# A feed-forward product of a fused transformer layer, with two of eight pairs of k-tiles in seven products for eight

## The chip, the cores and the metric

One core of a Trainium2 chip. The time is device microseconds of one execution; lower is better. The kernel before was run three times.

## The reference

One layer on 256 tokens of width 2048 in float32: an input projection, three kinds of attention, gates, an output projection, residual and layer norm, a feed-forward part, residual and layer norm, and a gated input. What the change touches is the feed-forward part (D = 2048, F = 5632):

```python
a, b = jnp.split(h @ w_ffn_in, 2, axis=-1)
f = (jax.nn.silu(a) * b) @ w_ffn_out
h = layer_norm(ALPHA * h + f, ln2_g, ln2_b)
```

The split and the product with Silu are what the kernel's lines 835 to 844 compute: chunk c of the first half is paired with chunk 11 + c.

## The kernel before

**Products.** TensorE has float32 products in three passes: each operand is split into a high part (`ACT.activation` Copy into a rounded type, line 140) and a low part (`DVE.tensor_sub`, line 141), and lines 208 to 210 sum high x high, low x high and high x low into one PSUM bank. The activations are stationary (128 k-rows by 128 tokens), the weights stream, 512 columns at a time. `gemm` loads weights in groups of two k-tiles (512 KB, line 151) through three `raw` buffers, splits them into four `whi` and four `wlo` buffers, and runs each group for both token halves. So ScalarE and VectorE do one split of 128x1024 for each 12 matmuls.

**Around the norms** a list of `LONG1` to `LONG3` groups is finished one token half before the other, so that the norm of one half lies beside matmuls of the other. Groups beyond four in such a list take their split tiles from a spare pool (`spare`); it is the first group of the list that does. For chunk 0 of the feed-forward part that pool is `k4b` (line 836).

**The feed-forward part.** `hT` holds the normed input in d-major halves (eight tiles of the pool `k4`). For each of 11 chunks of 512 columns: a product, Silu into `g` (ScalarE, line 839), a second product, their product (VectorE, line 843), and for each token half four transposes on TensorE (`to_dmajor`, line 239), whose result is split into `actT` (`k4h`, `k4l`). `actT` stays in SBUF for all 44 k-tiles. The second product (`add_and_norm`, `ffn_out`) has four chunks of 44 k-tiles.

**Order.** Each engine works through one queue in order; the order of each is set when the program is built, by priorities that follow the program text and by when a tile of a pool is free. All weight loads go through SyncE's queue.

**PSUM.** Eight banks: four of the pool `acc`, four of `scp` (transposes and small products).

Of the kernel before, what the change touches and what calls it, by code (L numbers as in the profile page):

```python
# [52 lines left out]
# the attention part of w_in in chunks of columns that one PSUM bank holds  # L53
# [12 lines left out]
# shape-only constants, one array of P rows  # L66
# [51 lines left out]
def build(ctx: ExitStack, tc: tile.TileContext, A: dict):  # L118
# [37 lines left out]
    # Work on the side: generators whose steps go between the groups of a product; each  # L156
    # yields how many groups its next step waits.
# [55 lines left out]

    class Halves:
        """d-major activations [P, n, S] in halves, in tiles of four blocks."""
# [13 lines left out]
        def put(self, k, n, half, src, hi_from=None):  # L229
            """Blocks k..k+n-1 of one token half from src [P, n, P]."""  # L230
# [4 lines left out]
    def to_dmajor(X, k0, src, half):  # L235
        """src [P tokens, 512] -> four blocks of X."""
        tp = sc_tile()
        for i in range(4):
            PE.transpose(tp[:, i * P:(i + 1) * P], src[:, i * P:(i + 1) * P], ident)  # L239
        X.put(k0, 4, half, tp.rearrange("p (n t) -> p n t", n=4))  # L240
# [13 lines left out]
    with ExitStack() as at:  # L254
# [16 lines left out]
        def load_x(k):  # L271
            """x^T up to block k, as the first product comes to it."""
# [562 lines left out]
    for c in range(11):  # L835
        ps = gemm(A["ffn_in"][c], hT, KT, 512, sizes=[[2] * LONG3] if c == 0 else (), spare=[k4b] * (LONG3 - 4))
        a = g_tile()
        for h in range(2):
            ACT.activation(a[:, h, :], ps[h], AF.Silu)  # L839
# [71 lines left out]
```

## Time and profile before

| | |
|---|---|
| runs, us | 1628.68, 1626.96, 1627.76 (median 1627.76) |
| the profiled execution: span, us | 1627.7 |
| TensorE busy | 99% of the span, granted clock 0.999 |
| VectorE, ScalarE busy | 56%, 45% |
| DMA | 310 MB, mean 191 GB/s |

The profile gives the span of one execution, from its first to its last instruction; no other time of that execution is listed, and the span is equal to the median of the runs. Busy time is that of instructions running, not waiting; a matmul is listed with its whole length, 0.39 us, though the next one starts after 0.23 us, so for TensorE the starts in the timeline are what counts. In the timeline, a bracket gives the idle time before an instruction and what ended it.

### The profile page before, as it was taken

How to read it: one execution, taken by the hardware profiler on the slowest of the kernel's cores; microseconds unless marked ns; L12 is line 12 of the kernel's file. 1: busy time of each engine (PE TensorE's matmuls, PEld its weight loads, DVE VectorE, ACT ScalarE, POOL GpSimd, SP SyncE). 2: the span in 40 equal slices, each digit the busy share in tenths (PEclk: the TensorE clock that was granted, in tenths of full speed). 3: DMA queues.
4: the chain of work that ended last, by engine and by line, in shares of the span. 5: the costliest groups of instructions: out<-in, count | busy, mean ns of one | idle time of the engine just before them, and what ended most of it. 6: DMA issues, size and time to landing. Idle time of an engine off the chain costs nothing. (4 is left out here: it accounts for less than half of the span.)

```text
span 1627.7 us, 19843 instructions
## 1 busy us (share of the span) xinstructions
PE 1612.1 (99%) x7581; PEld 1348.2 (83%) x7581; DVE 909.0 (56%) x1183; ACT 733.5 (45%) x917; POOL 17.9 (1%) x38
## 2 busy tenths in 40 slices
PE   9999999999999999999999999999999999999998
PEld 7777899988888888888888888888888888888787
DVE  5679765554646464556755454454454545545764
ACT  5455555554444444444444444444444433433343
POOL 1000000010000000000000000000000100000000
PEclk9999999999999999999999999999999999999999
DMA  7664653567666666677466666666666766666474
GB/s 261 183 193 154 208 160 111 168 205 228 192 193 185 194 193 192 191 232 222 150 196 191 186 193 193 184 192 187 189 190 193 234 194 194 194 194 198 148 232 131
DMA packets 90158, 310.26 MB, mean 191 GB/s; under 512 B 10320, under 2 KB 11472, under 8 KB 90064
## 3 DMA queue, kind: packets, MB, share of 16 engines
q1 hardware_dynamic: 88784, 304.81, 62.1%
q0 software_dynamic: 1280, 4.20, 0.9%
q8 instruction: 59, 0.97, 0.2%
q14 instruction: 35, 0.29, 0.1%
HBM read 306.86 MB, written 2.10 MB: 190 GB/s over the span
## 5 line engine op out<-in xcount | busy, mean ns | idle before, releaser
L141 DVE TENSOR_TENSOR wlo<-raw,whi 128x1024 fp32r<-128x1024 f32 (+2 forms) x572 | 683.1, 1196 | 668.4 <-ACT whi L140 663.9
L140 ACT ACTIVATE whi<-raw 128x1024 fp32r<-128x1024 f32 (+2 forms) x572 | 593.4, 1038 | 790.6 <-PE acc L209 680.0
L208 PE MATMUL acc<-whi,k4h 128*128 128x512 f32 (+2 forms) x2220 | 856.1, 386 | 2.2 <-ACT k4h L140 1.3
L210 PE MATMUL acc<-wlo,k4h 128*128 128x512 f32 (+2 forms) x2220 | 850.8, 383 | 2.1 <-DVE wlo L141 2.1
L209 PE MATMUL acc<-whi,k4l 128*128 128x512 f32 (+2 forms) x2220 | 851.3, 383 | 0.6 <-DVE k4l L141 0.6
L208 PEld LDWEIGHTS acc<-whi,k4h 128*128 128x128 f32 x2220 | 417.5, 188 | 81.4 <-ACT k4h L140 2.3
L210 PEld LDWEIGHTS acc<-wlo,k4h 128*128 128x128 f32 x2220 | 417.2, 188 | 78.9 <-DVE wlo L141 3.1
L209 PEld LDWEIGHTS acc<-whi,k4l 128*128 128x128 f32 x2220 | 417.5, 188 | 76.5 <-DVE k4l L141 1.3
L140 ACT ACTIVATE k4h<-sc 128x512 fp32r<-128x512 f32 (+1 forms) x62 | 33.2, 538 | 29.5 <-PE sc L239 22.3
L141 DVE TENSOR_TENSOR k4l<-sc,k4h 128x512 fp32r<-128x512 f32 (+1 forms) x62 | 36.4, 615 | 5.2 <-ACT k4h L140 5.0
L360 ACT ACTIVATE p<-p,nm 128x128 f32<-128x128 f32 (+1 forms) x40 | 17.8, 446 | 10.0 <-DVE nm L358 10.0
L239 PE MATMUL sc<-ident,g 128*128 128x128 f32 x120 | 19.1, 283 | 1.1 <-DVE g L843 1.1
L239 PEld LDWEIGHTS sc<-ident,g 128*128 128x128 f32 x120 | 12.6, 140 | 7.4 <-DVE g L843 4.1
L251 ACT ACTIVATE g<-acc 128x512 f32<-128x512 f32 x24 | 14.1, 589 | 5.8 <-PE acc L210 5.8
L734 DVE TENSOR_TENSOR g<-g,acc 128x512 f32<-128x512 f32 x24 | 16.4, 684 | 0.4
L571 PE MATMUL sc<-wlo,blk 128*30 128x256 f32 x64 | 15.7, 279 | 0.4 <-DVE wlo L141 0.4
L570 PE MATMUL sc<-whi,blk 128*30 128x256 f32 x64 | 16.0, 283 | 0.0
L140 ACT ACTIVATE wh<-raw 128x1024 fp32r<-128x1024 f32 x9 | 9.6, 1062 | 13.7 <-PE acc L209 5.2
L839 ACT ACTIVATE g<-acc 128x512 f32<-128x512 f32 x22 | 12.9, 589 | 5.3 <-PE acc L210 5.3
L843 DVE TENSOR_TENSOR g<-g,acc 128x512 f32<-128x512 f32 x22 | 15.0, 683 | 0.3
L209 PE MATMUL acc<-wh,k4l 128*128 128x512 f32 x36 | 14.3, 398 | 0.3 <-DVE k4l L141 0.2
L141 DVE TENSOR_TENSOR wl<-raw,wh 128x1024 fp32r<-128x1024 f32 x9 | 11.0, 1223 | 6.3 <-ACT wh L140 6.3
(209 smaller groups left out, 530.6 us busy)
## 6 DMA issues: line engine op xcount, KB each, us to landing
raw<-ffn_in SPq DMA_DIRECT2D x176, 512.0 KB, 3.6
raw<-gate SPq DMA_DIRECT2D x96, 512.0 KB, 3.6
raw<-ffn_out SPq DMA_DIRECT2D x88, 512.0 KB, 4.2
raw<-att_c SPq DMA_DIRECT2D x40, 512.0 KB, 4.4
raw<-att_f SPq DMA_DIRECT2D x48, 384.0 KB, 3.3
raw<-w_out SPq DMA_DIRECT2D x32, 512.0 KB, 4.2
raw<-ple_gate SPq DMA_DIRECT2D x32, 512.0 KB, 4.3
raw<-cmp SPq DMA_DIRECT2D x16, 512.0 KB, 4.3
```

Source lines behind the costliest of these rows:

```text
L140: ACT.activation(hi, src, AF.Copy)
L141: DVE.tensor_sub(lo, src, hi.bitcast(F32))
L208: PE.matmul(o, xh[:, c], h, start=(k == 0), stop=False)
L209: PE.matmul(o, xl[:, c], h, start=False, stop=False)
L210: PE.matmul(o, xh[:, c], l, start=False, stop=(k == kt - 1))
L239: PE.transpose(tp[:, i * P:(i + 1) * P], src[:, i * P:(i + 1) * P], ident)
L251: ACT.activation(G[name][:, h, :], ps[h], AF.Sigmoid)
L360: ACT.activation(p[:, c], p[:, c], AF.Exp, bias=nm[:, h:h + 1], scale=-1.0, accum_out=rs[:, h:h + 1])
L570: PE.matmul(ph[:2 * NCMP, :256], b, hi[:, l, :], start=first, stop=False)
L571: PE.matmul(ph[:2 * NCMP, :256], b, lo[:, l, :], start=False, stop=last)
L734: DVE.tensor_mul(g[:, h, :], g[:, h, :], ps[h])
L843: DVE.tensor_mul(a[:, h, :], a[:, h, :], ps[h])
```

## The change

Chunk 0 stays as it was (its spare tiles now come from `k4`). Chunks 1 to 10 take both their products at once, in `pair_gemm`: a 2 x 2 block product of two token halves by two chunks of columns (a is chunk c, b is chunk 11 + c), in pairs of k-tiles. Six of the eight pairs do the four block products of two k-tiles each, 24 matmuls. In pairs 2 and 4 (`SEVEN`) the two k-tiles are the inner dimension of a 2 x 2 by 2 x 2 block product, and seven products with sums of blocks (the Winograd form of Strassen's scheme) take the place of eight: 21 matmuls. The sums of activation blocks are made once, behind the first norm (`keep_pairs`, `Forms.put`); those of the weights for each chunk on VectorE (lines 276 to 278), from 1 MB of weights in `raw8`; those of the results at the end of pair 4 and of the chunk (lines 295 to 303). Four banks sum the four outputs, and the other four the products that several outputs share; the two pools swap roles from chunk to chunk.

For room the activations are not kept in SBUF: each chunk's are copied out of PSUM whole (line 967), stored to DRAM (line 969), and the first chunk of the second product loads them and splits them (`act_first`, lines 978 to 982). The pool `k4b` is closed before chunk 0 and the pool `fw` of `pair_gemm` stands in its place; a new one opens behind it.

```diff
+SEVEN = (2, 4)
...
+        def put(self, p, raw):
+
+            i = self.at[p]
+            if i // 2 == len(self.t):
+                self.t.append(tuple(self.pool.tile([P, 8, P], F32R, name=f"xf{x}", tag="k4") for x in "hl"))
+            a = [[raw[:, k, h * P:(h + 1) * P] for k in range(2)] for h in range(2)]
+            s = self.pool.tile([P, 4, P], F32, name="xs", tag="k4")
+            DVE.tensor_add(s[:, 0, :], a[1][0], a[1][1])
+            DVE.tensor_sub(s[:, 1, :], s[:, 0, :], a[0][0])
+            DVE.tensor_sub(s[:, 2, :], a[1][0], a[0][0])
+            DVE.tensor_sub(s[:, 3, :], a[0][1], s[:, 1, :])
+            j = 4 * (i % 2)
+            halves(s, *(t[:, j:j + 4, :] for t in self.t[i // 2]))
...
+    def pair_gemm(a, b, X, F, kt, pool, banks):
...
+        own, other = banks
+        c = [[own() for _ in range(2)] for _ in range(2)]
...
+        for p in range(np_):
+            raw = pool.tile([P, 4, 512], F32, name="raw8", bufs=3)
+            nc.sync.dma_start(raw[:, 0:2, :], b[:, 2 * p:2 * p + 2, :])
+            nc.sync.dma_start(raw[:, 2:4, :], a[:, 2 * p:2 * p + 2, :])
+            x = [[tuple(t[:, hs[h]] for t in X(2 * p + k)) for k in range(2)] for h in range(2)]
+            if p not in F.at:
+                w = [split(raw[:, 2:4, :], "", wp, 2), split(raw[:, 0:2, :], "", wp, 2)]
+                for h in range(2):
+                    for j in range(2):
+                        for k in range(2):
+                            product(c[h][j], x[h][k], w[j][k], p == 0 and k == 0, p == np_ - 1 and k == 1)
+                tick()
+                continue
+            t = [wp.tile([P, 1024], F32, name="raw", bufs=3).rearrange("p (k w) -> p k w", k=2) for _ in range(2)]
+            DVE.tensor_tensor(t[0], raw[:, 0:1, :].broadcast_to([P, 2, 512]), raw[:, 1:3, :], op=ALU.subtract)
+            DVE.tensor_sub(t[1][:, 0, :], raw[:, 1, :], t[0][:, 1, :])
+            DVE.tensor_sub(t[1][:, 1, :], raw[:, 3, :], t[1][:, 0, :])
+            b22, b11, b21 = split(raw[:, 1:4, :], "d", pool, 3, bufs=1)
+            t3, t1 = split(t[0], "t", pool, 2)
+            t2, t4 = split(t[1], "t", pool, 2)
+            first, stop = not m, p == last
...
+            product(m[1], x[0][0], b11, first, stop)
+            product(c[0][0], x[0][1], b21)
+            product(c[0][1], F(p, 3), b22)
+            product(m[7], F(p, 2), t3, first, stop)
+            product(m[5], F(p, 0), t1, first, stop)
+            product(m[6], F(p, 1), t2, first, stop)
+            product(c[1][0], x[1][1], t4)
+            if stop:
+                e = [g_tile(), g_tile()]
+                ACT.copy(e[0][:, 0, :], m[1])
+                DVE.tensor_add(e[0][:, 1, :], e[0][:, 0, :], m[6])
+                DVE.tensor_add(e[1][:, 0, :], e[0][:, 1, :], m[7])
+                DVE.tensor_add(e[1][:, 1, :], e[1][:, 0, :], m[5])
+                DVE.tensor_add(e[0][:, 1, :], e[0][:, 1, :], m[5])
+            tick()
+        for h in range(2):
+            for j in range(2):
+                DVE.tensor_add(e[h][:, j, :], e[h][:, j, :], c[h][j])
+        return e
...
+    part.close()
+    spilled = []
+    with tc.tile_pool(name="fw", bufs=2) as fw:
+        for c in range(11):
+            banks = (sc_tile, acc_tile) if c % 2 else (acc_tile, sc_tile)
+            if c == 0:
...
+            else:
+                e = pair_gemm(A["ffn_in"][c], A["ffn_in"][11 + c], hT, F, KT, fw, banks)
+                for h in range(2):
+                    ACT.activation(e[h][:, 0, :], e[h][:, 0, :], AF.Silu)
+                    DVE.tensor_mul(e[h][:, 0, :], e[h][:, 0, :], e[h][:, 1, :])
+                g = [e[h][:, 0, :] for h in range(2)]
+            t = k4.tile([P, 4, S], F32, name="act", tag="k4")
+            for h in range(2):
+                to_dmajor(None, 4 * c, g[h], h, lambda h, k0, tp: ACT.copy(t[:, :, h * P:(h + 1) * P], tp), banks[0])
+            d = dram.tile([P, 4, S], F32, name="actd")
+            nc.sync.dma_start(d, t)
+            spilled.append(d)
...
+    def act_first(k):
+
+        while len(actT.t) <= k // 4:
+            c = len(actT.t)
+            raw = wp.tile([P, 1024], F32, name="raw", bufs=3)
+            raw = raw.rearrange("p (k t) -> p k t", k=4)
+            nc.sync.dma_start(raw, spilled[c])
+            actT.add(k4 if 3 <= c < 7 else k4b)
+            halves(raw, *actT.t[c])
+        return actT(k)
```

**Where instructions stand.** The first place is TensorE's queue at the first feed-forward product, before (`wh4_6718` and `wl4_6719` are the split first weights of chunk 0, in spare tiles):

```order
L210 MATMUL acc_6476<-wlo_6521,k4h_5925 128x512
L208 MATMUL acc_6715<-wh4_6718,k4h_6575 128x512
L209 MATMUL acc_6715<-wh4_6718,k4l_6576 128x512
L210 MATMUL acc_6715<-wl4_6719,k4h_6575 128x512
...
L209 MATMUL acc_6715<-whi_6736,k4l_6578 128x512
L239 MATMUL sc_6681<-ident_73,y_5945 128x128 x4
L210 MATMUL acc_6715<-wlo_6737,k4h_6577 128x512
L239 MATMUL sc_6690<-ident_73,y_5946 128x128 x4
```

and the same place with the change (`wh4_6747`, `wl4_6748` are the same weights):

```order
L212 MATMUL acc_6478<-wlo_6523,k4h_5927 128x512
L331 MATMUL sc_6687<-ident_73,y_5947 128x128 x4
L331 MATMUL sc_6696<-ident_73,y_5948 128x128 x4
L331 MATMUL sc_6706<-ident_73,y_5949 128x128 x4
L331 MATMUL sc_6716<-ident_73,y_5950 128x128 x4
L210 MATMUL acc_6744<-wh4_6747,k4h_6577 128x512
L211 MATMUL acc_6744<-wh4_6747,k4l_6578 128x512
L212 MATMUL acc_6744<-wl4_6748,k4h_6577 128x512
```

All sixteen transposes of the second token half's norm now stand ahead of the product that had them among its matmuls. On ScalarE the split of those first weights stood ahead of every copy of the first token half's norm:

```order
L140 ACTIVATE whi_6520<-raw_6519 128x1024
L140 ACTIVATE wh4_6718<-raw_6717 128x1024
L140 ACTIVATE k4h_6575<-sc_6590 128x4x128
L140 ACTIVATE k4h_6577<-sc_6599 128x4x128
L140 ACTIVATE whi_6724<-raw_6723 128x1024
```

and with the change (`xc` are the whole copies of pairs 2 and 4, `xfh` the high halves of their sums):

```order
L142 ACTIVATE k4h_6581<-sc_6706 128x4x128
L936 COPY xc_6608<-sc_6696 128x2x128
L142 ACTIVATE k4h_6583<-sc_6716 128x4x128
L936 COPY xc_6619<-sc_6706 128x2x128
L142 ACTIVATE xfh_6723<-xs_6725 128x512
L142 ACTIVATE wh4_6747<-raw_6746 128x1024
L142 ACTIVATE xfh_6723<-xs_6732 128x512
```

The split of the first weights moved behind the second token half's norm, the copies and the first sums. The next place is VectorE's queue at the end of a chunk; with the change (raw_7987 is pair 7, raw_8049, raw_8084 and raw_8119 are pairs 0, 1 and 2 of the next chunk):

```order
L143 TENSOR_TENSOR wlo<-raw_7987,whi 128x1024 x2
L143 TENSOR_TENSOR wlo<-raw_8049,whi 128x1024 x2
L303 TENSOR_TENSOR g<-g,sc 128x512
L276 TENSOR_TENSOR raw<-raw_8119 128x1024
L303 TENSOR_TENSOR g<-g,sc 128x512 x2
L963 TENSOR_TENSOR g<-g 128x512
L303 TENSOR_TENSOR g<-g,sc 128x512
L143 TENSOR_TENSOR wlo<-raw_8084,whi 128x1024
L963 TENSOR_TENSOR g<-g 128x512
L143 TENSOR_TENSOR wlo<-raw_8084,whi 128x1024
```

Where two multiplications stood between weights, four sums and two multiplications now stand, with two weights of the next chunk ahead of them and a difference and a weight among them. The last place is VectorE's queue at the end of chunk 10 (line 143 with `k4l<-raw` is a reloaded tile of activations):

```order
L143 TENSOR_TENSOR wlo<-raw_10297,whi 128x1024 x2
L143 TENSOR_TENSOR k4l<-raw,k4h 128x1024
L143 TENSOR_TENSOR wlo<-raw,whi 128x1024 x2
L303 TENSOR_TENSOR g<-g,acc 128x512 x2
L963 TENSOR_TENSOR g<-g 128x512
L303 TENSOR_TENSOR g<-g,acc 128x512
L143 TENSOR_TENSOR wlo<-raw,whi 128x1024
L303 TENSOR_TENSOR g<-g,acc 128x512
L143 TENSOR_TENSOR k4l<-raw,k4h 128x1024
L963 TENSOR_TENSOR g<-g 128x512
```

A second reloaded tile stands ahead of the last multiplication. On TensorE the eight transposes of chunk 10 stand ahead of the second product's first matmul; in chunks 1 to 9 the first four stand two matmuls and the other four eleven matmuls into the next chunk (one matmul in each case behind chunk 0).

## Rows read from the trace of the kernel before

**Rows 1.** The page's first part: busy us, share of the span, instructions.
```profile
PE 1612.1 (99%) x7581; PEld 1348.2 (83%) x7581; DVE 909.0 (56%) x1183; ACT 733.5 (45%) x917; POOL 17.9 (1%) x38
```

**Rows 2.** Windows, one chunk: busy us by engine, granted clock, DMA share, GB/s.
```profile
864.50:909.00 44.50, 44.50 (x201) 36.72 (x200) 22.04 (x21) 19.14 (x20) 0.00 (x0) 1.00 0.64 189
```

**Rows 3.** Timeline of TensorE within a product: start us, us, instruction.
```profile
904.75 0.39 PE L208 MATMUL acc<-whi,k4h 128*128 128x512 f32 x1
...
917.67 0.39 PE L208 MATMUL acc<-whi,k4h 128*128 128x512 f32 x1
```

**Rows 4.** Timeline of ScalarE, Silu of the first token half, two chunks.
```profile
858.35 0.60 ACT L839 ACTIVATE g<-acc 128x512 f32<-128x512 f32 x1 [0.53 <-PE acc L210]
...
902.91 0.60 ACT L839 ACTIVATE g<-acc 128x512 f32<-128x512 f32 x1 [0.53 <-PE acc L210]
```

**Rows 5.** Timeline of TensorE at a chunk's transposes.
```profile
881.27 0.39 PE L208 MATMUL acc<-whi,k4h 128*128 128x512 f32 x1
881.50 0.65 PE L239 MATMUL sc<-ident,g 128*128 128x128 f32 x4
881.91 0.48 PE L209 MATMUL acc<-whi,k4l 128*128 128x512 f32 x1
```

**Rows 6.** Timeline of TensorE from the output projection's end through the norm.
```profile
790.71 0.39 PE L210 MATMUL acc<-wlo,k4h 128*128 128x512 f32 x1
790.93 0.39 PE L208 MATMUL acc<-wh,k4h 128*128 128x512 f32 x1
...
796.16 0.63 PE L239 MATMUL sc<-ident,y 128*128 128x128 f32 x4
...
801.77 0.63 PE L239 MATMUL sc<-ident,y 128*128 128x128 f32 x4
```

**Rows 7.** Timeline of VectorE in the same stretch.
```profile
795.27 1.41 DVE L786 SCALAR_TENSOR_TENSOR y<-y,rstd,gb 128x512 f32<-128x512 f32 x2
796.60 0.74 DVE L785 SCALAR_TENSOR_TENSOR y<-y,mv,gb 128x512 f32<-128x512 f32 x1
```

**Rows 8.** Groups of instructions by shape: busy us, mean ns of one, idle before.
```profile
L141 DVE TENSOR_TENSOR wlo<-raw,whi 128x1024 fp32r<-128x1024 f32 x507 | 620.4, 1225 | 613.9 <-ACT whi L140 609.8 <-PE acc L209 2.4 <-PE acc L210 1.3
L140 ACT ACTIVATE whi<-raw 128x1024 fp32r<-128x1024 f32 x507 | 538.0, 1061 | 735.7 <-PE acc L209 652.9 <-DMA raw<-att_c 17.6 <-DMA raw<-ffn_out 11.6
L141 DVE TENSOR_TENSOR k4l<-sc,k4h 128x512 fp32r<-128x512 f32 x46 | 29.9, 684 | 1.0 <-ACT k4h L140 0.7
L140 ACT ACTIVATE k4h<-sc 128x512 fp32r<-128x512 f32 x46 | 27.1, 593 | 24.0 <-PE sc L239 22.3
L335 DVE TENSOR_TENSOR ra<-acc,cst 128x128 f32<-128x128 f32 x2 | 0.6, 288 | 0.0
```

**Rows 9.** Timeline of TensorE at the start of the kernel.
```profile
10.13 0.70 PE L208 MATMUL acc<-whi,k4h 128*128 128x482 f32 x2 [1.34 <-ACT k4h L140]
11.41 0.49 PE L209 MATMUL acc<-whi,k4l 128*128 128x482 f32 x1 [0.57 <-DVE k4l L141]
...
12.39 0.54 PE L210 MATMUL acc<-wlo,k4h 128*128 128x482 f32 x1
12.73 0.61 PE L209 MATMUL acc<-whi,k4l 128*128 128x482 f32 x1
...
15.54 0.54 PE L210 MATMUL acc<-wlo,k4h 128*128 128x482 f32 x1
15.92 0.38 PE L208 MATMUL acc<-whi,k4h 128*128 128x482 f32 x1
```

**Rows 10.** Windows of that stretch, columns as in rows 2.
```profile
13.00:14.00 1.00, 1.00 (x4) 0.79 (x4) 0.89 (x2) 0.89 (x2) 0.00 (x0) 0.50 0.98 392
14.00:15.00 1.00, 1.00 (x4) 0.86 (x3) 1.00 (x2) 0.28 (x1) 0.00 (x0) 0.50 1.01 248
```

**Rows 11.** DMA issues: count, KB each, median us from issue to landing.
```profile
raw<-ffn_in SPq DMA_DIRECT2D x176, 512.0 KB, 3.6
raw<-ffn_out SPq DMA_DIRECT2D x88, 512.0 KB, 4.2
gb<-ln_g POOLq DMA_DIRECT2D x8, 256.0 KB, 6.9
```

**Rows 12.** Timeline of ScalarE while the second norm's parameters are loaded.
```profile
1276.51 1.06 ACT L140 ACTIVATE whi<-raw 128x1024 fp32r<-128x1024 f32 x1 [4.18 <-DMA raw<-ffn_out]
```

**Rows 13.** Windows of the same stretch, columns as in rows 2.
```profile
1270.00:1285.00 15.00, 13.88 (x66) 11.38 (x65) 8.35 (x9) 6.42 (x7) 2.12 (x4) 1.00 0.91 296
```

More of the change, by code (lines that the diff above doesn't have):

```diff
@@ L212, in gemm, with __init__, __call__ @@
         return ps
+    class Forms:
+        def __init__(self, pool, pairs):
+            self.at, self.t, self.pool = {p: i for i, p in enumerate(pairs)}, [], pool
+        def put(self, p, raw):
[10 more added lines that the diff above has]
+            halves(s, *(t[:, j:j + 4, :] for t in self.t[i // 2]))
+        def __call__(self, p, j):
+            i = self.at[p]
+            return tuple(t[:, 4 * (i % 2) + j, :] for t in self.t[i // 2])
@@ new lines, in pair_gemm, with product, split @@
+    def pair_gemm(a, b, X, F, kt, pool, banks):
+        own, other = banks
+        c = [[own() for _ in range(2)] for _ in range(2)]
+        m = {}
+        hs = [slice(0, P), slice(P, S)]
+        np_, last = kt // 2, max(F.at)
+        def product(o, x, w, first=False, stop=False):
+            (xh, xl), (h, l) = x, w
+            PE.matmul(o, xh, h, start=first, stop=False)
+            PE.matmul(o, xl, h, start=False, stop=False)
+            PE.matmul(o, xh, l, start=False, stop=stop)
+        def split(src, name, pool, n, **kw):
+            hi, lo = (pool.tile([P, n, 512], F32R, name=f"w{name}{x}", tag=f"w{name}{x}", **kw) for x in ("hi", "lo"))
+            halves(src, hi, lo)
+            return [(hi[:, i, :], lo[:, i, :]) for i in range(n)]
+        for p in range(np_):
[19 more added lines that the diff above has]
+            first, stop = not m, p == last
+            for n in (1, 5, 6, 7):
+                if first:
+                    m[n] = other()
+            product(m[1], x[0][0], b11, first, stop)
[17 more added lines that the diff above has]
+        return e
@@ L786, in layer_norm, with add_and_norm @@
             DVE.scalar_tensor_tensor(y, y, rstd, gb[n][:, 1, :], op0=ALU.mult, op1=ALU.add)
[L787 to L789 removed]
+            to_dmajor(T, 4 * n, y, h, raw)
+    def add_and_norm(src, X, kt, old, params_of, extra, T, long, spare, raw=None, first=None):
         stats = new_stats()
@@ L794, in add_and_norm @@
             if n < 3:
-                ps = gemm(src[n], X, kt, 512)
+                ps = gemm(src[n], first if first and n == 0 else X, kt, 512)
                 for h in range(2):
@@ L828, in build, with keep_pairs @@
     later = Later(k4)
+    F = Forms(k4, SEVEN)
+    copies = {}
+    def keep_pairs(h, k0, blocks):
+        for p in range(k0 // 2, k0 // 2 + 2):
+            if p in F.at:
+                if h == 0:
+                    copies[p] = k4.tile([P, 2, S], F32, name="xc", tag="k4")
+                ACT.copy(copies[p][:, :, h * P:(h + 1) * P], blocks[:, 2 * p - k0:2 * p - k0 + 2, :])
     add_and_norm(A["w_out"], mixT, KT, x_tile, lambda: params("ln1_g", "ln1_b", k4b),
-                 lambda: gated_input(k4, 0, ep), later, LONG1, [k4] * (LONG1 - 4))
+                 lambda: gated_input(k4, 0, ep), later, LONG1, [k4] * (LONG1 - 4), raw=keep_pairs)
@@ L831, in build @@
     hT = later.x
-    actT = Halves()
[L835 to L839, printed above, removed]
-        ps = gemm(A["ffn_in"][11 + c], hT, KT, 512)
-        actT.add(k4 if 3 <= c < 7 else k4b)
-        for h in range(2):
-            DVE.tensor_mul(a[:, h, :], a[:, h, :], ps[h])
-            to_dmajor(actT, 4 * c, a[:, h, :], h)
+    for p in SEVEN:
+        F.put(p, copies[p])
```

33 lines of the change are left out of this document (23 added, 10 removed).

## The prediction

> **What bounds the kernel now.** I read the share of busy time first: TensorE 99%, VectorE 56%, ScalarE 45% [rows 1]. So time falls only where TensorE gets less to do, and rises wherever it is made to wait. Then the feed-forward stretch alone: in one chunk of 44.5 us TensorE is busy throughout at the full granted clock, VectorE 22.0 us, ScalarE 19.1 us, the DMA engines at 0.64 [rows 2]. The matmuls of 128x512 start 57 in 12.92 us, one every 0.2267 us [rows 3]. A chunk (one Silu to the next, [rows 4]) lasts 44.56 us: 192 matmuls are 43.53; two sets of four transposes, each of which lengthens the step between two matmuls from 0.23 to 0.64 us [rows 5], are 0.82; 0.2 us is waiting. VectorE's work is hidden completely there, but it has an order, and TensorE's order names the places where it waits for it. These places decide.
>
> **What the change removes.** In chunks 1 to 10 two of eight pairs take 21 instead of 24 matmuls: 10 x 2 x 3 = 60 fewer, 60 x 0.2267 = **-13.6 us**. That is all it can give.
>
> **The first norm.** Before, the first feed-forward product starts 0.22 us behind the last matmul of the output projection, at 790.93, and fills the time that the second token half's norm takes; the norm's four sets of transposes lie among its matmuls, the last at 801.77 [rows 6]. With the change TensorE's order has all sixteen transposes ahead of that product, and the product's first weights are split on ScalarE and VectorE behind the copies and sums for the seven products. I walk VectorE's new order from a point that is the same in both, the third scaling at 796.60 [rows 7], with the durations of [rows 7, 8]: two scalings 1.48 (798.1); three times "low half 0.68" around two shifts of 0.74 (801.6); three sums of 128x128, priced by the nearest row, 0.29 each (802.5); a weight 1.23 (803.7); a low half 0.68 and a sum 0.29 (804.7); ScalarE's high half of the sums 0.59 (805.3) and the low half 0.68 (806.0); four sums (807.1); the awaited weight 1.23: **808.3**. The product's third matmul needs it; before, it ran at 791.4. That is 16.9 us late, less the four sets of transposes that now lie in the gap, 4 x 0.41: **+15.2 us**. Below, with the sums free and no handover, 12.3; above, with 0.2 us at each of ten handovers, 17.2. Nothing else can cover it: every later matmul stands behind in the same queue.
>
> **The clock behind the gap.** At the start of the trace TensorE waited 1.34 and 0.57 us, and from 12.39 to 15.9 nine matmuls started 0.40 instead of 0.22 us apart [rows 9], with a granted clock of 0.50, the 1.2 GHz level [rows 10]: 1.6 us lost. A gap of 15 us I charge the same: **+1.6** (0 to 3.2, if it comes at the gap of the next paragraph but one too). The Trainium skill, page TensorE: Matmul & The Clock Gate, Part 1, says that the throttled clock is the default and only activity releases it. This trace agrees at its start; applied to both gaps the rule would make the sum 1645 instead of 1643.5.
>
> **Nine chunk boundaries.** A chunk now asks of VectorE 12 x 1.23 for ordinary weights, 2 x (three of 1.23, two of 0.68 and one of 1536 columns, 1.77 by the step from 512 to 1024 columns) for the seven products, eight sums and two products of 0.68: 35 us of 44, and its idle time in my walk is about 8 us, so the bulk is hidden. At the boundary it is not. The four weight buffers hold two pairs, so the next chunk's first weights wait for pair 6, whose second buffer is freed 24 x 0.2267 = 5.4 us before the chunk's end T. ScalarE 1.06, VectorE 1.23: -3.0. Behind it in VectorE's order: a sum (-2.3), the first difference of the next seven products 1.23 (-1.1), two sums (+0.3), the product (+1.0). The first transposes stand two matmuls behind T, at +0.45, and wait 0.6. Then a sum, a weight and the second product: 3.6, where the transposes would stand at 3.5. Together 0.8 against 0.2 now: 0.6 x 9 = **+5.4 us** (0 if the buffers come free earlier, 18 at 2 us each).
>
> **Into the second product.** Behind chunk 10 all eight transposes stand ahead of the next matmul. VectorE then does, from -3.0: two sums, a product (-0.9), a sum, a weight whose buffer is freed at -1.4 (+1.0), a sum (1.7), the low half of a reloaded tile (2.9), the product (3.6). TensorE is done with the first four transposes at 0.4: **+3.2 us** (1.5 without the reloaded tile and with the weight ready, 5.5 if that tile lands late).
>
> **The reload.** The first of four chunks of the second product takes 11 loads of 512 KB beside its 22 weights, through the same three buffers. Two weights and one reload take one turn of them: landing 3.6 to 4.2 us [rows 11], split 1.06 and 1.23, so 5.9 to 6.5 us, while TensorE uses them up in 24 x 0.2267 = 5.4. It starts four groups ahead (10.9 us). Carried through nine turns this ends with no wait at 3.6 and 3.8 us at 4.2. The norm's parameters, eight loads of 256 KB on POOL's queue (2.1 MB), come somewhere near; before, they held ScalarE up for 4.2 us [rows 12], with the DMA engines at 0.91 [rows 13]. I take **+4** (0 to 12). The Trainium skill, page DMA: Bandwidth & Descriptors, Specifications, puts a core's HBM limit at about 358 GB/s; 19.4 MB would then need, as an estimate, 54 of the chunk's 60 us, nothing would wait, and the sum would be 1639.5. A row here even shows 392 GB/s at a share of 0.98 [rows 10].
>
> The activations' stores (11 of 512 KB) I cost at nothing: the queue moves 189 GB/s in a chunk now [rows 2]. SyncE holds each store until its copy is done, about 5 us behind T, with only loads behind it whose tiles are needed over 5 us later; without that slack it would be a microsecond a chunk, inside the bound of the boundaries.
>
> **Sum.** -13.6 + 15.2 + 1.6 + 5.4 + 3.2 + 4 = +15.8 on the profiled 1627.7 us, which is the median of the runs (1627.76) to 0.1: **1643.5 us**, slower by 1.0%.
>
> **Rivals.**
> (a) *Faster: the norm's gap closes.* The place is the first product's first weight tile. If TensorE got it by about 799, with all else at its lower end (-13.6 + 6 + 1.5), the result is 1622 to 1624. For it: the sums are small and the weights were loaded long before. Against: the wait is in three queues' order at once, and even with the product running beside them the last transposes came at 801.77 [rows 6]. It decides at a gap of 8 us where my lower bound is 12.3. Chance 0.05.
> (b) *No change:* gain and gap cancel and the boundaries cost nothing: -13.6 + 12.3 + 1.5 to 3, some 1628 to 1631. Chance 0.09.
> (c) *VectorE becomes the bound:* 35 us of work in bursts of 6.8 us for each seven products, against 4.8 us of matmuls. For it: its single weight buffer for the differences and its long order with ScalarE. Against: 8 us of slack in a chunk. At 2.5 us a chunk instead of 0.6, +17: about 1660. Chance 0.14.
> (d) *The reload is DMA-bound:* 12 us instead of 4, and a fall of the clock with it: about 1653. Chance 0.12.
> (e) *The change doesn't do what it says.* The new order shows 21 matmuls at both pairs of ten chunks; I give it nothing.
> My own sum has 0.60.
>
> **Numbers.** A measurement of this kernel can tell about 0.2% (3.3 us) from no change. All terms at their lower ends give 1628, at their upper ends 1670; leaving out the outer parts of (a), (b) and (c) on either side, the range is **1631 to 1661**. Faster is (a), 0.05; same is (b), 0.09; slower is the rest, 0.86.
>
> **What would show it.** Right: TensorE idle, but for transposes, from about 791 to 806-808, with one or more matmuls at 0.4 us after; chunks of about 43.8 us; a gap of 3 us at the last chunk's end; the second product's first chunk some 64 us long instead of 60. Wrong: chunks at 44.5 or above would mean that VectorE, not the matmul count, sets them; a first product that starts before 800 would break the largest term.

## The result and the profile after

The changed kernel takes 1640.46 us (median of 4 runs, 1638.28 to 1641.39) against 1627.77 us: a ratio of 1.0071, 95% interval 1.0057 to 1.0085. The forecast was 1643.5 us and slower by 1.0%. The profiled execution took 1641.39 us, its span is 1639.3 us. So a run's time is not its span: here it is 2.1 us above it, and as much in a second trace of the kernel before (1630.26 against 1628.1). The span of 1627.7 us, from which the forecast starts, and the median of the runs are the same number but not the same quantity. The change is +12.7 us by the medians and +11.6 us by the two spans.

The page's first part, as [rows 1]:

```profile
PE 1607.8 (98%) x7521; PEld 1342.2 (82%) x7521; DVE 1037.7 (63%) x1342; ACT 774.2 (47%) x964; POOL 17.9 (1%) x38
```

The 60 matmuls are gone (7581 to 7521), and TensorE's share fell all the same. Where, the timelines show. First TensorE at the norm, as [rows 6] (start us, us, instruction, idle before and who ended it):

```profile
788.14 0.39 PE L212 MATMUL acc<-wlo,k4h 128*128 128x512 f32 x1
794.17 1.94 PE L331 MATMUL sc<-ident,y 128*128 128x128 f32 x8 [5.65 <-DVE y L884]
797.42 1.09 PE L331 MATMUL sc<-ident,y 128*128 128x128 f32 x4 [1.31 <-DVE y L884]
798.68 1.09 PE L331 MATMUL sc<-ident,y 128*128 128x128 f32 x4 [0.17 <-DVE y L884]
804.06 0.80 PE L210 MATMUL acc<-wh,k4h 128*128 128x512 f32 x1 [4.29 <-ACT wh L142]
...
805.91 0.79 PE L212 MATMUL acc<-wl,k4h 128*128 128x512 f32 x1 [0.63 <-DVE wl L143]
...
809.92 0.63 PE L212 MATMUL acc<-wlo,k4h 128*128 128x512 f32 x1
810.35 0.56 PE L210 MATMUL acc<-whi,k4h 128*128 128x512 f32 x1
```

The projection's last matmul, at 788.14, is followed by transposes alone. It ends, counted as one step of 0.22 us after its start, at 788.36; the product's third matmul starts at 805.91, 17.55 us later. Behind that one, matmuls step by 0.43 us until 810.35. VectorE there, as [rows 7]:

```profile
800.38 1.22 DVE L143 TENSOR_TENSOR wlo<-raw,whi 128x1024 fp32r<-128x1024 f32 x1
...
803.10 0.69 DVE L143 TENSOR_TENSOR xfl<-xs,xfh 128x512 fp32r<-128x512 f32 x1 [0.70 <-ACT xfh L142]
...
804.64 1.22 DVE L143 TENSOR_TENSOR wl<-raw,wh 128x1024 fp32r<-128x1024 f32 x1
```

An ordinary weight (`wlo`) is split at 800.38; the one that TensorE's order wants first (`wl`, the group in spare tiles) comes behind both sets of sums. The windows of the same place (columns as in [rows 2]):

```profile
800.00:805.00 5.00, 0.94 (x2) 0.50 (x2) 4.27 (x12) 2.48 (x5) 0.00 (x0) 0.50 0.93 329
805.00:810.00 5.00, 4.37 (x11) 3.22 (x11) 1.46 (x2) 0.39 (x1) 0.00 (x0) 0.50 0.92 336
810.00:815.00 5.00, 5.00 (x22) 4.09 (x21) 0.00 (x0) 1.05 (x1) 0.00 (x0) 0.93 0.41 158
```

The granted clock is 0.50, the 1.2 GHz level, and comes back behind 810. The Silu of chunk 1 and of chunk 10, as [rows 4]:

```profile
892.30 0.61 ACT L962 ACTIVATE g<-g 128x512 f32<-128x512 f32 x1
...
1281.33 0.63 ACT L962 ACTIVATE g<-g 128x512 f32<-128x512 f32 x1 [1.89 <-DVE g L303]
```

Nine chunks in 389.03 us are 43.23 us each, against 44.56. TensorE into the second product:

```profile
1283.62 0.39 PE L255 MATMUL acc<-wlo,k4h 128*128 128x512 f32 x1
1283.85 0.60 PE L331 MATMUL acc<-ident,g 128*128 128x128 f32 x4
1287.17 0.66 PE L331 MATMUL acc<-ident,g 128*128 128x128 f32 x4 [2.73 <-DVE g L963]
1287.60 0.47 PE L210 MATMUL acc<-whi,k4h 128*128 128x512 f32 x1
...
1288.63 0.63 PE L211 MATMUL acc<-whi,k4l 128*128 128x512 f32 x1
...
1291.62 0.56 PE L212 MATMUL acc<-wlo,k4h 128*128 128x512 f32 x1
1292.02 0.40 PE L210 MATMUL acc<-whi,k4h 128*128 128x512 f32 x1
```

A wait of 2.73 us, and then eight matmuls from 1288.63 to 1292.02, 0.42 us apart: a second fall of the clock (granted 1.00 from 1287 to 1288, 0.50 from 1288.6 to 1292.0). Later in the same chunk, at the reloaded tiles:

```profile
1334.83 0.50 PE L211 MATMUL acc<-whi,k4l 128*128 128x512 f32 x1 [0.76 <-DVE k4l L143]
```

The wait shown is only a part: the step from the matmul before, at 1333.60, is 1.23 us instead of 0.23. Nine longer steps between 1327.4 and 1349.5 lose 5.2 us, and behind them eight matmuls again step by 0.43 (granted clock 0.50 from 1350 to 1353).

**The balance**, from the trace of before to that of after, by three marks (the projection's last matmul, the end of chunk 0, the end of chunk 10's matmuls) and the 264th matmul of the second product:

| stretch | before | after | change | forecast |
|---|---|---|---|---|
| up to the projection's last matmul | 790.71 | 788.14 | -2.6 | 0 |
| chunk 0 with the norm | 46.0 | 63.2 | +17.2 | 15.2 + 1.6 |
| chunks 1 to 10 | 10 x 44.54 | 10 x 43.25 | -12.9 | -13.6 + 5.4 |
| into and through the second product's first chunk | 62.1 | 72.2 | +10.1 | 3.2 + 4 |
| the rest | 283.4 | 283.2 | -0.2 | 0 |

The sum is +11.6, as the spans have it (1639.3 - 1627.7).

### The profile page after: what moved, and what is told of

It is laid out like the page before. It is cut to its first block, busy times and chain, and to the rows that moved or that the text cites. A ratio compares the mean times of both kernels' runs of the same rounds, so it can differ in the third digit from the quotient of the medians.

```text
span 1639.3 us, 19963 instructions
## 1 busy us (share of the span) xinstructions
PE 1607.8 (98%) x7521; PEld 1342.2 (82%) x7521; DVE 1037.7 (63%) x1342; ACT 774.2 (47%) x964; POOL 17.9 (1%) x38
## 5 line engine op out<-in xcount | busy, mean ns | idle before, releaser
L210 PE MATMUL acc<-whi,k4h 128*128 128x512 f32 (+3 forms) x1580 | 609.0, 386 | 2.6 <-ACT k4h L142 2.1
L211 PE MATMUL acc<-whi,k4l 128*128 128x512 f32 (+3 forms) x1580 | 603.3, 382 | 3.3 <-DVE k4l L143 3.3
L212 PE MATMUL acc<-wlo,k4h 128*128 128x512 f32 (+3 forms) x1580 | 602.3, 381 | 2.1 <-DVE wlo L143 2.1
L212 PEld LDWEIGHTS acc<-wlo,k4h 128*128 128x128 f32 x1580 | 298.0, 189 | 54.9 <-DVE wlo L143 2.6
L255 PE MATMUL acc<-wlo,k4h 128*128 128x512 f32 x240 | 94.4, 393 | 0.0
L255 PE MATMUL sc<-wlo,k4h 128*128 128x512 f32 x240 | 94.3, 393 | 0.0
L254 PE MATMUL sc<-whi,k4l 128*128 128x512 f32 x240 | 93.6, 390 | 0.0
L254 PE MATMUL acc<-whi,k4l 128*128 128x512 f32 x240 | 93.5, 390 | 0.0
L253 PE MATMUL acc<-whi,k4h 128*128 128x512 f32 x240 | 93.4, 389 | 0.0
L253 PE MATMUL sc<-whi,k4h 128*128 128x512 f32 x240 | 93.4, 389 | 0.0
L255 PEld LDWEIGHTS acc<-wlo,k4h 128*128 128x128 f32 x240 | 45.0, 188 | 9.0
L143 DVE TENSOR_TENSOR wdlo<-raw,wdhi 128x1536 fp32r<-128x1536 f32 x20 | 35.1, 1754 | 11.6 <-ACT wdhi L142 11.0
```

The costliest lines, as they stand in the source:

```text
L210: PE.matmul(o, xh[:, c], h, start=(k == 0), stop=False)
L211: PE.matmul(o, xl[:, c], h, start=False, stop=False)
L212: PE.matmul(o, xh[:, c], l, start=False, stop=(k == kt - 1))
L253: PE.matmul(o, xh, h, start=first, stop=False)
L254: PE.matmul(o, xl, h, start=False, stop=False)
L255: PE.matmul(o, xh, l, start=False, stop=stop)
```

## Experiments

Every run stands beside runs of the kernel before on its own chip; ratios are to those (a hundredth of a per cent is 0.16 us). On these chips the kernel before took 1629.6 to 1630.5 us in the median, single runs 1625.6 to 1634.4, so its stretches in the traces say more than the medians. Three stretches are used: **A**, from the projection's last matmul to chunk 1's first (46.0 us in the kernel before); **B**, a chunk, as a mean over chunks 1 to 10; **C**, from the end of chunk 10's matmuls to the end of the 264th matmul of the second product (62.1 us). Each is read from one trace. A second trace of the kernel before (e9) has A 46.1, B 44.54 and C 64.5: A and B repeat, but C differs by 2.4 us between two traces of one kernel.

| kernel | ratio, 95% interval | A | B | C |
|---|---|---|---|---|
| the change | 1.0071, 1.0057 to 1.0085 | 63.2 | 43.25 | 72.2 |
| e1 sums late | 0.9992, 0.9982 to 1.0003 | 50.6 | 43.22 | 70.8 |
| e2 no spare tile | 0.9998, 0.9988 to 1.0008 | 47.9 | 43.58 | 70.9 |
| e3 = e1 + banks swapped | 0.9994, 0.9985 to 1.0002 | 49.7 | 43.17 | 69.1 |
| e4 = e1 + an eighth product | 1.0079, 1.0067 to 1.0092 | 49.8 | 44.49 | 71.8 |
| e5 = e3 without reload | 0.9924, 0.9912 to 0.9936 | 50.1 | 43.22 | 60.8 |
| e6 = e3 + reload in own tiles | 0.9999, 0.9987 to 1.0010 | 50.8 | 43.28 | 71.6 |
| e7 the change, gap filled | 1.0075, 1.0061 to 1.0090 | 63.7 | 43.17 | 71.5 |
| e8 = e6, three pairs | 0.9966, 0.9953 to 0.9979 | 53.4 | 42.60 | 71.0 |
| e10 = e6 + early reload | 0.9973, 0.9960 to 0.9986 | 50.6 | 43.25 | 67.2 |
| e11 = e10, three pairs | 0.9920, 0.9906 to 0.9935 | 52.6 | 42.57 | 63.1 |
| e12 = e10, four pairs | 0.9926, 0.9913 to 0.9939 | 47.4 | 42.91 | 70.0 |

### The gap at the norm: e1, e2

e1 moves the sums behind chunk 0's two products:

```
-    for p in SEVEN:
-        F.put(p, copies[p])
...
                 g = [g[:, h, :] for h in range(2)]
+                for p in SEVEN:
+                    F.put(p, copies[p])
```

> Only the place of the sums of the activations (Forms.put for both pairs) moves: from ahead of chunk 0 of the feed-forward part to behind its two products. Theory A (the gap at the first norm comes from the order: the first weights of chunk 0 are split behind the copies and sums, so the product that used to lie beside the norm stands behind it): the gap of 17.5 us and the 2 us of slow matmuls behind it go, the time is 1640.5 - 15.2 - 2 = about 1623.5, below the kernel before by some 4 us; TensorE goes on 0.2 us behind the projection's last matmul. Rival B (the norm itself holds TensorE, because the copies for the seven products lengthen its chain): at least 8 us of the gap stay, the time is 1632 or more. Rival C (VectorE has no room for the sums in chunk 0 or 1 either): the gap goes, but a wait of 5 us or more turns up in chunk 1.

1627.94 us, where 1623.5 was expected. TensorE from the projection's end, and at the end of chunk 0:

```profile
791.32 0.39 PE L212 MATMUL acc<-wlo,k4h 128*128 128x512 f32 x1
791.64 0.50 PE L210 MATMUL acc<-wh,k4h 128*128 128x512 f32 x1
...
793.62 0.50 PE L212 MATMUL acc<-wl,k4h 128*128 128x512 f32 x1 [1.24 <-DVE wl L143]
...
841.51 0.66 PE L331 MATMUL acc<-ident,g 128*128 128x128 f32 x4 [2.62 <-DVE g L955]
```

The gap and the slow matmuls behind it are gone, which rules out rival B, the norm itself; stretch A fell by 12.6 us, not by 17. It kept a wait for the low half of the spare weight (1.24) and got a new one at chunk 0's end (2.62), where the change has none: rival C in a smaller form. VectorE there:

```profile
838.50 1.22 DVE L143 TENSOR_TENSOR wlo<-raw,whi 128x1024 fp32r<-128x1024 f32 x1
839.64 1.22 DVE L143 TENSOR_TENSOR wtlo<-raw,wthi 128x1024 fp32r<-128x1024 f32 x1
840.77 0.68 DVE L955 TENSOR_TENSOR g<-g,acc 128x512 f32<-128x512 f32 x1
```

It works without a break at weights of chunk 1, and the product that the transposes wait for stands behind them.

e2 leaves the sums where they are and takes the spare tile away:

```
-                ps = gemm(A["ffn_in"][c], hT, KT, 512, sizes=[[2] * LONG3], spare=[k4] * (LONG3 - 4))
+                ps = gemm(A["ffn_in"][c], hT, KT, 512, sizes=[[2] * 4])
```

> The sums stay where the change put them, ahead of chunk 0; but chunk 0's first list has four groups of weights instead of five, so that none of them takes a spare tile of the pool k4, behind the tiles of the sums. If the order of tiles of that one pool is what holds the first weights (theory A in its narrower form), this alone brings the product back in front of the transposes: about 1624, as with the sums moved, perhaps 1 us more, because the cover is 24 matmuls and not 30. If the sums hold up ScalarE and VectorE wherever the tile lies (rival D), the gap stays at over 8 us and the time at 1632 or more.

1629.15 us: 1.2 us above e1, which the runs of the two can't tell from nothing, and 5 us above the 1624 expected. The trace shows the product back in front of the transposes, its 24 matmuls without a break behind the projection (A 47.9; a wait of 2.02 us for chunk 0's product falls into chunk 1, which takes 46.9):

```profile
793.44 0.39 PE L212 MATMUL acc<-wlo,k4h 128*128 128x512 f32 x1
794.88 1.29 PE L331 MATMUL sc<-ident,y 128*128 128x128 f32 x8 [1.05 <-DVE y L884]
```

So it is not the work of the sums that cost 15 us, but that one weight's tile, the first that TensorE wants, came behind the sums' tiles in the same pool.

### What a matmul is worth: e4

```
             product(c[1][0], x[1][1], t4)
+            product(c[1][0], x[1][1], t4)
```

> The sums behind chunk 0, and each of the 20 places with seven products does its last product twice (24 matmuls instead of 21, the second of its halves a repetition, so the output is not the reference's). All work of the other engines stays. Theory A (a chunk's time is its matmuls; the sums on VectorE are hidden, the boundaries cost nothing): 60 x 0.2267 = 13.6 us more than with the sums moved alone, about 1637. Rival F (VectorE or the weights' buffers set the chunk's time, and the measured 1.3 us a chunk is only part of what is there to be gained): the added matmuls fill waits, and it is less than 10 us more.

1642.23 us, 14.3 more than e1 (13.6 expected); a chunk takes 44.48 instead of 43.23 us by its Silus, 1.25 where six matmuls are 1.36. The matmuls' price stands: VectorE did not set these chunks.

### Into the second product: e3, e5, e6

e3, on top of e1:

```
-            banks = (sc_tile, acc_tile) if c % 2 else (acc_tile, sc_tile)
+            banks = (acc_tile, sc_tile) if c % 2 else (sc_tile, acc_tile)
```

> The sums behind chunk 0, as above, and the two pools of PSUM banks change places in every chunk, so that chunk 10 sums in the banks of scp and the second product finds two free banks of acc. Theory A: the wait of 2.7 us into the second product is one for banks of acc (chunk 10 holds all four until its last sums); the second product's first matmuls stand ahead of the transposes again, and the wait and the 1.6 us of matmuls at the slow clock go: 4 us less than with the sums moved alone, about 1619.5. Rival E: what holds the second product is the reloaded tile and its split; then a wait of 2 us or more stays there and the time is within 1 us of the run before this one.

1627.78 us: no difference from e1 that can be told. The wait itself did go:

```profile
1272.48 0.39 PE L255 MATMUL sc<-wlo,k4h 128*128 128x512 f32 x1
1272.71 0.60 PE L331 MATMUL sc<-ident,g 128*128 128x128 f32 x4
1273.07 0.47 PE L210 MATMUL acc<-whi,k4h 128*128 128x512 f32 x1
...
1276.12 0.60 PE L331 MATMUL sc<-ident,g 128*128 128x128 f32 x4
```

The second product's matmuls now lie between the two sets of transposes, with no wait and no slow matmul behind. So the wait of 2.73 us was one for banks of `acc`, not for the reload. But C fell by only 1.7 us, less than two traces of one kernel differ: TensorE came sooner to the reloaded tiles and waited there instead, from 1301 on.

e5 takes stores and reload out of e3 and splits a tile that lies in SBUF:

```
-            d = dram.tile([P, 4, S], F32, name="actd")
-            nc.sync.dma_start(d, t)
-            spilled.append(d)
...
-            raw = wp.tile([P, 1024], F32, name="raw", bufs=3)
-            raw = raw.rearrange("p (k t) -> p k t", k=4)
-            nc.sync.dma_start(raw, spilled[c])
+            raw = E[0].rearrange("p h (k t) -> p (h k) t", k=2)
```

> The kernel with the sums late and the banks swapped, without the stores of the activations and without their reload: the eleven splits into halves stay, but they read a tile that lies in SBUF (so the second product has other activations). In the kernel with the banks swapped the second product's first chunk takes 68.7 us for 264 matmuls, whose bare time is 264 x 0.2267 = 59.9 us; with a set of transposes on each half, 60.7. Theory A (the loads are late: three buffers of raw tiles, shared by weights and reloads): the chunk falls to about 61 us and the time by 8 us, to about 1620. Rival G (the splits themselves, one more for every two weights on ScalarE and VectorE, are what is late): the chunk stays above 66 us and the time within 3 us.

1616.61 us, ratio 0.9924: C is 60.8 us, the bare matmuls and transposes. The splits are hidden; the loads cost 8 us behind an entry without a gap. (The medians of e3 and e5, on two chips, lie 11.2 us apart; behind the projection the traces differ by 7.5, so the rest is not shown to be the reload.) This is also what the change, with the edits of e3, could gain if the activations could stay in SBUF.

e6 gives e3's reloads tiles of their own:

```
-            raw = wp.tile([P, 1024], F32, name="raw", bufs=3)
-            raw = raw.rearrange("p (k t) -> p k t", k=4)
+            raw = k4.tile([P, 4, S], F32, name="ra", tag="k4")
```

> The kernel with the sums late and the banks swapped; the reloads land in tiles of the pool k4, which is half empty then, instead of in the three raw buffers of the weights. The bytes and the splits stay. Theory A (buffers, not bytes: 19.4 MB in 61 us is 318 GB/s, and the trace has shown 392 GB/s in a microsecond): the first chunk of the second product takes 61 to 64 us instead of 68.7 and the time is 1620 to 1623. Rival H (the bytes: the DMA engines are full there): the chunk stays above 66 us, with the DMA share at 0.95 or above through it, and the time within 3 us.

1629.76 us, no gain. The first chunk itself just met the expectation (64.0 us from its first matmul), but its start did not:

```profile
1277.88 0.66 PE L331 MATMUL sc<-ident,g 128*128 128x128 f32 x4 [2.77 <-DVE g L963]
1282.15 1.22 PE L210 MATMUL acc<-whi,k4h 128*128 128x512 f32 x2 [3.61 <-ACT k4h L142]
```

SyncE's queue and ScalarE tell why:

```profile
1270.03 1.69 SPq L153 DMA_DIRECT2D raw<-ffn_out  x2
...
1275.52 0.33 SPq L153 DMA_DIRECT2D raw<-ffn_out  x1
...
1275.90 0.90 SPq L979 DMA_DIRECT2D ra<-actd  x2
...
1281.04 1.06 ACT L142 ACTIVATE k4h<-ra 128x1024 fp32r<-128x1024 f32 x1 [1.88 <-DMA ra<-actd]
```

The first reload, which the first matmul needs, was issued behind three weights at 1275.90; nothing runs until it lands and is split. So the chunk's 64.0 us are no clean sign for buffers and against bytes: its first matmul came 7.6 us behind chunk 10, and the loads behind the first had that time.

### The clock: e7

```
             to_dmajor(T, 4 * n, y, h, raw)
+            if h and raw:
+                pw = sc_tile().rearrange("p (n t) -> p n t", n=4)
+                m = T.t[0][0][:, :, 0:P]
+                for _ in range(26 if n == 3 else 5):
+                    PE.matmul(pw, m[:, 0, :], m, start=True, stop=True)
```

> The changed kernel itself, with 41 matmuls of 128x512 into a bank that nobody reads, put in TensorE's order between and behind the second token half's transposes at the first norm, so that TensorE has work in the gap. Nothing that anyone waits for changes. If the slow matmuls behind the gap come from TensorE's idleness in it, the granted clock stays at 1.00 through the gap, the product's first matmuls step by 0.23 instead of 0.43 us, and about 2 us go: 0.9988 of the changed kernel's time, 1.006 of the kernel before. The product's third matmul still stands 17 to 18 us behind the projection's end, since what it waits for is VectorE's order. If the clock falls for another reason, the steps of 0.43 us stay and nothing is gained.

1640.33 us, ratio 1.0075: nothing gained. TensorE at the projection's end and at the fill's end, and the window of the fill's last part:

```profile
790.05 0.39 PE L212 MATMUL acc<-wlo,k4h 128*128 128x512 f32 x1
...
804.23 6.17 PE L890 MATMUL sc<-k4h 128*128 128x512 f32 x26
810.24 0.39 PE L210 MATMUL acc<-wh,k4h 128*128 128x512 f32 x1
...
810.69 0.39 PE L212 MATMUL acc<-wl,k4h 128*128 128x512 f32 x1
```

```profile
805.00:810.00 5.00, 5.00 (x23) 4.13 (x22) 4.18 (x9) 2.36 (x4) 0.00 (x0) 1.00 0.90 304
```

Ahead of the product the granted clock is 1.00, and its matmuls step by 0.23, as expected. Through the gap it did not stay there (0.55 from 795 to 800): the first fillers ran at the slow clock (five in 2.48 us), in front of the next transposes. And the third matmul came 20.4 us behind the projection's end (790.28) instead of 17.55: its weight was ready 18.4 us behind it, at 808.63, and the last 26 fillers ran until 810.24, 1.6 us too long. So the fill moved the slow matmuls and cost 2.9 us of waiting; A is 63.7 instead of 63.2 us, so the clean steps gave back 2.4, about what the slow steps in the change cost. That TensorE's idleness ahead goes with the slow clock behind this gap is shown.

### The trace before, a second time: e9

> The kernel before, unchanged, for a second trace. In the first one the output projection's last matmul stood at 790.71; in the changed kernel and in every experiment so far at 788.0 to 788.2, although the order of all engines is the same up to there; the difference lay in the first 20 us (34 matmuls in 10 to 20 us at a granted clock of 0.83, against 43 at 1.00). If that is chance of one execution, this trace shows the last matmul at another place than 790.7, probably near 788; if it belongs to the kernel, at 790.7 again.

1630.26 us. The expectation has a false number in it: 788.0 to 788.2 were other rows of the projection; its last matmul stood at 791.32 in e1, 791.25 in e3 and 789.18 in e5. Here it is at 789.32, and 10 to 20 us have 42 matmuls at a clock of 1.00. So 788 to 791 is what one and the same beginning takes, and the -2.6 us in the balance are chance. This trace shows a second thing, at the entry of the second product:

```profile
1283.10 0.65 PE L239 MATMUL sc<-ident,g 128*128 128x128 f32 x4 [1.94 <-DVE g L843]
```

Six matmuls at 0.43 us follow it (granted clock 0.50 from 1284.4 to 1287.0). In the first trace the wait there is 1.12 us, with no slow matmul behind. So the kernel before can lose time there too, and the +10.1 in the balance would be +7.7 against this trace.

### A version that beats both: e8, e10, e11, e12

e8 is e6 with `SEVEN = (1, 3, 5)`.

> The kernel with the reloads in tiles of their own, and three pairs of k-tiles in seven products (1, 3 and 5) instead of two (2 and 4): 30 matmuls fewer, and for each of ten chunks about 4.4 us more of VectorE's work (6.8 for a pair in seven products against 2.5 for an ordinary one), 39 of a chunk's 42 us. Theory A (as long as VectorE has room, a removed matmul is worth its 0.2267 us): a chunk of 42.5 us instead of 43.2, 6.8 us less than the run before this one. Rival F (at this load VectorE's order sets the chunk): chunks of 43 us or more and no gain.

1623.94 us, 5.8 below e6. Chunks are 42.60 us.

e10 mends what e6 showed, with two edits:

```
+            if c == 10:
+                early = [k4.tile([P, 4, S], F32, name="ra", tag="k4") for _ in range(3)]
+                for i, t in enumerate(early):
+                    nc.sync.dma_start(t, spilled[i])
...
                 for h in range(2):
                     ACT.activation(g[:, h, :], ps[h], AF.Silu)
+                for p in SEVEN:
+                    F.put(p, copies[p])
                 ps = gemm(A["ffn_in"][11 + c], hT, KT, 512)
...
-                for p in SEVEN:
-                    F.put(p, copies[p])
...
-            raw = k4.tile([P, 4, S], F32, name="ra", tag="k4")
-            nc.sync.dma_start(raw, spilled[c])
+            if c < len(early):
+                raw = early[c]
+            else:
+                raw = k4.tile([P, 4, S], F32, name="ra", tag="k4")
+                nc.sync.dma_start(raw, spilled[c])
```

> The kernel with the reloads in tiles of their own (sums late, banks swapped), with two more edits: the first three reloads are issued ahead of chunk 10, and the sums stand between chunk 0's two products instead of behind them. In the run before, the first reload was issued behind three weight loads at 1275.90 and TensorE waited 2.8 and 3.6 us into the second product; chunk 0's transposes waited 2.7 us for VectorE. Theory A (all of these are places in a queue, none a lack of room): all three waits fall below 1 us, the first chunk of the second product stays at 63 us or below, and the time falls by about 8 us to 1621 to 1623, 0.995 of the kernel before. Rival H (the bytes): the waits come back at the reloads behind the third, and the time is 1626 or more.

1625.98 us: half of what was expected. The waits at the entry are gone (second product 0.23 us behind chunk 10). The wait at chunk 0's end stayed, 2.59 us: it comes with the sums ahead of chunk 0 (e2), between its products (here) and behind them (e1), so where they stand is not its cause; the run of chunk 1's weights shown at e1 is the likely one. And a later reload, the ninth, was late:

```profile
1317.17 1.06 ACT L142 ACTIVATE k4h<-ra 128x1024 fp32r<-128x1024 f32 x1 [5.81 <-DMA ra<-actd]
```

The reloads now occupy tiles of `k4` that the second norm's parameters want, so those come during the reload (1282 to 1308; in the changed kernel they were issued from 1263 to 1274). A reload's median time from issue to landing is 4.4 us in the changed kernel and 6.4 here.

In the window from 1275 to 1290 the DMA engines are at 0.96 and move 334 GB/s:

```profile
1275.00:1290.00 15.00, 15.00 (x70) 12.34 (x69) 8.87 (x8) 6.38 (x8) 1.11 (x2) 1.00 0.96 334
```

This is what rival H foresaw: a wait at a reload behind the third, a time of 1626, and engines at 0.96, then 0.86 and 0.88 up to 1320. But from 1260 to 1275 they were at 0.17 with 44 GB/s. Whether the bytes or the late issue of the loads decided here, these runs leave open.

e11 is e10 with `SEVEN = (1, 3, 5)`.

> The same with three pairs (1, 3, 5) in seven products. Theory A: 30 matmuls fewer, 5.8 to 6.8 us less than with two pairs, 1615 to 1617, 0.991 of the kernel before: faster than both kernels.

1618.10 us, ratio 0.9920: 13 us faster than the kernel before (10.6 to 15.3 by the interval), and by its ratio the fastest of all. C is 63.1 us; that it is 4 us shorter than e10's, beyond the chunks' own gain, was not expected. One difference is in the traces: from 1260 to 1275, where e10 moved 44 GB/s, e11 moved 210. That this is the cause was not tried.

e12 is e10 with `SEVEN = (1, 2, 4, 5)`.

> The same with four pairs (1, 2, 4, 5) in seven products. TensorE's bare time of a chunk is 180 x 0.2267 + 0.82 = 41.6 us; VectorE's work by the durations of its rows is 35 + 2 x 4.4 = 43.8 us. Here VectorE should become the bound: chunks of 43.5 to 45 us, no faster than with two pairs (43.2) and 15 us or more slower than with three. If instead the steps between VectorE's instructions, 0.08 us shorter than their durations, leave it room, chunks of 42 us and another 6 us less than with three pairs.

1618.45 us, level with e11. Neither number of the expectation was met: chunks of 42.91 us. VectorE's load in windows over the chunks of the two (third pair of numbers):

```profile
845.00:1260.00 415.00, 414.98 (x1867) 344.23 (x1866) 356.00 (x363) 232.21 (x234) 0.00 (x0) 1.00 0.61 211
```

```profile
840.00:1260.00 420.00, 418.35 (x1857) 341.01 (x1858) 396.88 (x408) 240.17 (x246) 0.00 (x0) 1.00 0.61 209
```

At 356.0 of 415 us busy (86%), a chunk is 0.3 us above its bare 183 x 0.2267 + 0.82 = 42.3. At 396.9 of 420 (94%) it is 1.3 above 41.6: 0.46 of that is one wait of 4.6 us, for chunk 0's product, that falls into chunk 1 here. Chunks 2 to 10 take 42.3, still 0.7 above; in two of them, at 896 and at 1023 us, TensorE loses 0.5 and 0.2 us in a wait for a low half (`wdlo`) that VectorE makes for the seven products. So the fourth pair's matmuls bring little: A and the ten chunks together take 1.8 us less than in e11, where 30 matmuls are 6.8, and C takes 7 us more.

## Why the prediction was right, and where its terms were off

The direction and the largest cause held, and the time lies in the range. Point by point:

- **Matmuls, -13.6: held.** 60 fewer on the page, a chunk shorter by 1.3 us, and e4 gave 14.3 us for putting them back.
- **The first norm, +15.2: held.** Its third matmul was forecast 17.4 us behind the projection's end (808.3 against 790.93) and came 17.55 behind. Without the gap it would have come 0.45 behind, and four sets of transposes, 1.6, left chunk 0's matmuls for the gap: 17.1 - 1.6 = 15.5. The nearness is in part luck: the walk began 0.6 us later behind the projection than forecast (the third scaling at 6.25 us instead of 5.67) and took 0.5 us less (11.25 instead of 11.75), since its rows overlap and one wait for ScalarE of 0.64 was not in it. "Nothing else can cover it" held for this order; e1 and e2 show how little undoes it.
- **Clock, +1.6: too small.** It was charged once; the trace has three falls, behind the norm, at the second product's entry and behind the reload, some eight to eleven matmuls each at 0.43 instead of 0.23 us: 2.3 + 1.6 + 1.6 = 5.5 us, above the upper bound of 3.2. By the Trainium skill (TensorE: Matmul & The Clock Gate, Part 1) the throttled clock is the default and activity releases it. The trace agrees at all three places, with a granted clock of 0.50 behind a stretch in which TensorE was idle in whole or in part; charging the second product's gap too, as the rule has it, would have brought this term to 3.2. But which short wait brings a fall these runs do not settle: 2.73 us at the entry brought one here, while the same wait at the same place in e7 (2.72 us; granted clock 1.00 from 1288 to 1292) and seven waits of 0.3 to 0.8 us at the reloads in e3 brought none. So the two smaller falls are in part chance.
- **Nine boundaries, +5.4: the step that failed.** The change measures about 0.07 us a chunk instead of 0.6: 1.29 us saved of 1.36, and seven of chunks 1 to 9 take 43.15 to 43.19 us, no more than the removed matmuls leave. The order of VectorE was as walked, its times were not:

```profile
1237.45 0.68 DVE L303 TENSOR_TENSOR g<-g,sc 128x512 f32<-128x512 f32 x1
1238.05 1.22 DVE L276 TENSOR_TENSOR raw<-raw 128x1024 f32<-128x1024 f32 x1
1239.19 1.28 DVE L303 TENSOR_TENSOR g<-g,sc 128x512 f32<-128x512 f32 x2
1240.38 0.68 DVE L963 TENSOR_TENSOR g<-g 128x512 f32<-128x512 f32 x1
```

```profile
1241.14 0.64 PE L331 MATMUL sc<-ident,g 128*128 128x128 f32 x4
```

The product was forecast to be done 1.0 us behind the chunk's end (1240.68); it was done at 1241.06, 0.4 behind, and the transposes, at 0.46, did not wait. A row's duration is not its step: 0.68 us rows follow each other at 0.60, 1.22 us rows at 1.14. Five rows of 0.08 make 0.4 us, and the walk had started 0.2 us late (by its own terms, -5.4 + 1.06 + 1.23, it starts at -3.15 and not at -3.0; measured is -3.2).
- **Into the second product, +3.2: held** at 2.73 us of waiting. That its cause is the banks was not in the prediction; e3 shows it.
- **The reload, +4: 5.2 us**, within its bounds, but not by its sum: nine turns of 6.5 us against 5.4 fall 9.5 us behind, less than the 10.9 us that the loads are ahead, so no wait follows from them at 4.2 us either. The chunk took 68.5 us from its first matmul, not 64. Rival (d), a DMA bound, did not come true in the change: from 1305 to 1350, where the waits are, the DMA engines were at 0.66 to 0.76 with 216 to 242 GB/s. That the loads were late is shown by e5; that it was the three shared buffers fits this share, but e6 and e10, which took the reloads out of them, brought other late loads and don't show it cleanly. The Trainium skill's limit (DMA: Bandwidth & Descriptors, Specifications) left no wait at all by the estimate; the trace had waits well below that rate, so in the change rate was not what decided.
- **Rival (c), VectorE the bound:** it was busy 270.8 of 350 us in the chunks, 77%, 33.5 us a chunk where 35 was forecast. e11 and e12 show between what loads it begins to bind: with VectorE at 86% a chunk is 0.3 us above its bare matmuls and transposes, at 94% it is 0.7 to 1.3 above.
- **Rival (a)** came true only with another order: e1 closes the gap; even so the time was 1627.9 us and not 1622 to 1624.

The errors cancel: clock 3.9 and reload 1.2 too little, boundaries 4.7 too much, 1.4 us that the first trace of the kernel before had lost in C itself (62.1 against 60.7 bare) and the forecast did not take off, and 2.6 us of the beginning that are no part of the change. So the total came out nearer than its terms, and that is luck.

## What to carry to other kernels

Before a step is put in front of a product that covers something else, look at the first tile which that product needs, and at what else allocates from the same pool: one weight behind two sets of small sums cost 15 us, more than all the removed matmuls gave. When work leaves the bound engine, its price is sure but its waits move: each gap closed here (e3, e6) reappeared at the next late load, and issuing three loads early (e10) won back half of what was expected. Walk a queue with the steps between rows, not with the rows' durations.

## What the runs showed of the hardware that was not expected

- VectorE's rows overlap by 0.08 us: a 128x128 sum lasts 0.28 us and the next begins 0.20 us later, a 128x512 product 0.68 and 0.60, a 128x1024 split 1.22 and 1.14.
- The granted clock fell not only behind the long gap but also behind a wait of 2.73 us at the second product's entry, and behind five waits of up to 0.9 us at the reloads. At the entry it was 1.00 through the wait and fell to 0.50 only 1.4 us after TensorE had gone on. Waits of the same kind and length brought no fall in other traces (2.72 us at the entry in e7, the reloads in e3).
- One and the same program's beginning (order and data unchanged) ended anywhere between 788.0 and 791.3 us.
